# Rotary embedding on one core: one unit's stores moved beside the loads, another's gathered into a single late transfer

## The chip, the cores and the metric

One core of a Trainium2 chip. The time is the device time of one execution in microseconds (us). A profiled execution's span is some 1.8 us shorter than its time. A run is called slow only when it lies over 1.5% above the fastest of its kernel.

A "unit" is 16 of the 64 heads: 4 MiB of float32, as 128 partitions of 8192 elements. There are four, numbered 0 to 3. X0 to X3 are their inputs in SBUF, OUT is the tile that is stored.

## The reference

```python
# x: (8, 8, 1024, 64) float32; freqs: 32; positions: 1024; scale 0.5
angles = np.outer(positions * scale, freqs)
cos, sin = np.cos(angles), np.sin(angles)
out_first  = x_first * cos - x_second * sin      # halves of the last axis
out_second = x_first * sin + x_second * cos
```

16.8 MB come in and 16.8 MB go out, all in float32. Little arithmetic is done per byte.

## The kernel before

GpSimd issues nearly all loads; they cast float32 to float16 on the way. Two quarters of unit 0 are loaded uncast, by SyncE and ScalarE. VectorE works in float16, ScalarE casts back to float32 into OUT, and the stores follow.

```python
    pin(nc.gpsimd.dma_start(out=Xf[0][:, :NH], in_=xv[0][:, :NH]))
    ...                                                   # (cut)
    for u in range(1, NU):
        c = C2 if u == NU - 1 else 0                      # C2 = 1024
        pin(nc.gpsimd.dma_start(out=Xf[u][:, : N - c], in_=xv[u][:, : N - c]))
        if c:
            pin(nc.gpsimd.dma_start(out=Xf[u][:, N - c :], in_=xv[u][:, N - c :]))
    ...                                                   # (cut: the sin/cos table T)
    for u in range(NU):                                   # NU = 4
        OUT = xout.tile([P, N], FP32, tag="O")            # three buffers
        for s in range(2):
            ...                                           # (cut: four VectorE instructions)
            pin(nc.scalar.copy(out=OUT[:, ns], in_=Xf[u][:, ns]))
            if u >= NU // 2:
                pin(nc.sync.dma_start(out=ov[u][:, ns], in_=OUT[:, ns]))
        if u < NU // 2:
            c = C1 if u == 0 else 0                       # C1 = 512
            if c:
                pin(nc.gpsimd.dma_start(out=ov[u][:, :c], in_=OUT[:, :c]))
            pin(nc.gpsimd.dma_start(out=ov[u][:, c:], in_=OUT[:, c:]))
```

So units 0 and 1 are stored by GpSimd, behind the loads in the same queue (q0), and units 2 and 3 in halves by SyncE (q1).

Of the kernel before, what the change touches and what calls it, by code (L numbers as in the profile page):

```python
# [21 lines left out]
def kernel(  # L22
# [8 lines left out]
    nc = tc.nc  # L31
    pin = tc.keep_in_program_order
# [9 lines left out]
    NU = NBH // HEADS  # L42
# [2 lines left out]
    K8 = S // P  # L45
    G = P // HP
    W = K8 * half
    C1 = 512
    C2 = 1024
    assert S % HP == 0 and D == 2 * half and NBH % HEADS == 0 and G * K8 == K  # L50

# [3 lines left out]
    ov = out.rearrange("b h s d -> (b h s d)").rearrange("(u p n) -> u p n", p=P, n=N)  # L55
# [34 lines left out]
        out=one, in_=one, compare_op=ALU.not_equal, fill=1.0, base=0,  # L90
        pattern=[[-1, G], [-G, HP]], channel_multiplier=1,
    ))
    for u in range(1, NU):
        c = C2 if u == NU - 1 else 0
# [11 lines left out]
        out=posf, in_=pos_i64.bitcast(I32).rearrange("p (k t) -> p k t", t=2)[:, :, 0]  # L106
# [3 lines left out]
        out=y,  # L110
# [8 lines left out]
        out=r, in0=m, scalar=_MAGIC, in1=y, op0=ALU.subtract, op1=ALU.subtract  # L119
# [5 lines left out]
        out=ra.bitcast(I32), in0=r.bitcast(I32), scalar1=0x7FFFFFFF, scalar2=None, op0=ALU.bitwise_and  # L125
# [5 lines left out]
    for g in range(0, G, 2):  # L131
        ps = spread.tile([P, 2, 2, W], FP32, tag="g")
        for i in range(2):
            nc.tensor.matmul(  # L134
                out=ps[:, i].rearrange("p t w -> p (t w)"),
# [12 lines left out]
    for u in range(NU):  # L148
        OUT = xout.tile([P, N], FP32, tag="O")
        for s in range(2):  # L150
            ks = slice(s * KH, (s + 1) * KH)
            ns = slice(s * NH, (s + 1) * NH)
            Xs = X[u][:, ks]
            sin_b = T[:, 0, ks].unsqueeze(2).broadcast_to((P, KH, 2, half))
            cos_b = T[:, 1, ks].unsqueeze(2).broadcast_to((P, KH, 2, half))
            pr = tmp.tile([P, KH, 2, half], FP16, tag="pr")
            pin(nc.vector.tensor_tensor(out=pr, in0=Xs, in1=sin_b, op=ALU.mult))  # L157
            pin(nc.vector.tensor_tensor(out=Xs, in0=Xs, in1=cos_b, op=ALU.mult))  # L158
            pin(nc.vector.tensor_tensor(  # L159
                out=Xs[:, :, 0, :], in0=Xs[:, :, 0, :], in1=pr[:, :, 1, :], op=ALU.subtract  # L160
            ))
            pin(nc.vector.tensor_tensor(  # L162
                out=Xs[:, :, 1, :], in0=pr[:, :, 0, :], in1=Xs[:, :, 1, :], op=ALU.add
            ))
            pin(nc.scalar.copy(out=OUT[:, ns], in_=Xf[u][:, ns]))  # L165
            if u >= NU // 2:
                pin(nc.sync.dma_start(out=ov[u][:, ns], in_=OUT[:, ns]))
        if u < NU // 2:
            c = C1 if u == 0 else 0
            if c:  # L170
                pin(nc.gpsimd.dma_start(out=ov[u][:, :c], in_=OUT[:, :c]))  # L171
            pin(nc.gpsimd.dma_start(out=ov[u][:, c:], in_=OUT[:, c:]))  # L172


# [1 line left out]
_INS = ['x', 'freqs', 'positions', 'scale']  # L176
_OUTS = [((8, 8, 1024, 64), 'float32')]
# [30 lines left out]
```

## Time and profile before

| | before |
|---|---|
| time, median of 3 (range) | 84.54 us (84.37 to 84.59) |
| span of the profiled execution | 82.7 us |
| DMA packets of the three queues, share of 16 engines' span | 97.2% |
| VectorE busy / ScalarE busy | 73% / 49% |
| last cast of ScalarE ends | 73.5 us |
| last store lands | 81.8 us |

Read the third row first: the sixteen DMA engines have hardly any free time. The chain on the page names VectorE, because it follows instructions and ends at the last cast, 8 us before the last store has landed. The lines themselves are in the prediction.

### The profile page before, as it was taken

The numbers are of one execution on the slowest core, as the hardware profiler recorded it, in microseconds if no ns is written. First come the engines' busy times: TensorE is split into PE (matmuls) and PEld (weight loads), VectorE is DVE, ScalarE is ACT, GpSimd is POOL, SyncE is SP. The second block draws the span as 40 slices with busy tenths as digits, with TensorE's granted clock in tenths as the row PEclk, the third lists the DMA queues.
The fourth block names the chain that finished last, engine by engine and source line by source line (L and its number), as shares of the span: only waits on it lengthen the run. The fifth ranks groups of instructions, "written<-read, shape, count | busy, mean of one in ns | idle before, by whom it ended". The sixth has DMA issues, their size and how long they took to land.

```text
span 82.7 us, 184 instructions
## 1 busy us (share of the span) xinstructions
PE 6.4 (8%) x18; PEld 2.4 (3%) x18; DVE 60.3 (73%) x40; ACT 40.1 (49%) x18; POOL 5.7 (7%) x16
## 2 busy tenths in 40 slices
PE   0011798200000000000000000000000000000000
PEld 0011232000000000000000000000000000000000
DVE  0306276999999999999999999999999997000000
ACT  0602159999960691294089049309705912950000
POOL 4950000000020002000000200000000000000000
PEclk9999999995555555555555555555555555555555
DMA  3899998996998999999499889989899899999991
GB/s 55 323 323 269 297 325 186 254 254 135 246 254 182 198 254 222 222 222 222 36 456 446 357 386 476 507 357 460 380 523 404 365 428 428 460 404 436 428 428 79
DMA packets 2099, 26.22 MB, mean 317 GB/s; under 512 B 371, under 2 KB 371, under 8 KB 563
## 3 DMA queue, kind: packets, MB, share of 16 engines
q0 software_dynamic: 1088, 15.73, 66.7%
q1 hardware_dynamic: 720, 9.44, 27.3%
q10 hardware_dynamic: 290, 1.06, 3.2%
q14 instruction: 1, 0.00, 0.0%
HBM read 16.79 MB, written 16.78 MB: 406 GB/s over the span
## 4 chain that ended last, share of the span: by engine, by line
DVE 54%; ACT 14%; issue 7%; DMA 6%; PE 5%; DVEq 1%; ACTq 0%
DVE X L158 19%; DVE pr L157 19%; DVE X L162 9%; DMA freq_row<-in_freqs_dram 6%; ACT T L144 5%; DVE X L159 5%; ACT OUT L165 4%; PE ps L134 4%; ACT X L145 4%; DVEq L203 1%; PE cfreq L102 1%; ACT tab L127 1%; DVE r L118 1%; DVE y L109 1%; ACTq L71 0%
## 5 line engine op out<-in xcount | busy, mean ns | idle before, releaser
L165 ACT CAST OUT<-X 128x4096 f32<-128x4096 f16 x8 | 28.8, 3605 | 24.2 <-DVE X L162 24.2
L157 DVE TENSOR_TENSOR pr<-X,T 128x4096 f16<-128x4096 f16 x8 | 18.3, 2292 | 1.0 <-ACT T L144 0.7
L158 DVE TENSOR_TENSOR X<-X,T 128x4096 f16<-128x4096 f16 x8 | 18.3, 2292 | 0.3
L159 DVE TENSOR_TENSOR X<-X,pr 128x2048 f16<-128x2048 f16 x8 | 9.8, 1225 | 0.3
L162 DVE TENSOR_TENSOR X<-pr,X 128x2048 f16<-128x2048 f16 x8 | 9.7, 1218 | 0.0
L144 ACT CAST T<-ps 128x1024 f16<-128x1024 f32 x6 | 5.7, 1030 | 2.6 <-PE ps L134 2.6
L134 PE MATMUL ps<-tab,sel 128*128 128x512 f16 x16 | 5.8, 503 | 2.6 <-ACT tab L127 2.2
L142 DVE CAST T<-ps 128x1024 f16<-128x1024 f32 x2 | 2.4, 1224 | 2.2 <-PE ps L134 2.2
L145 ACT CAST X<-X0f 128x4096 f16<-128x4096 f32 x1 | 3.6, 3650 | 0.0
L100 DVE COPY sel<-one 128x2048 f16<-128x2048 f16 x1 | 0.7, 694 | 2.8 <-POOL one L89 2.8
L122 ACT ACTIVATE tab<-r 128x256 f16<-128x256 f32 x1 | 0.4, 416 | 4.4 <-DVE r L118 4.4
L172 POOL DMA_DIRECT2D out_dram<-OUT x2 | 1.1, 531 | 20.2 <-ACT OUT L165 20.2
L122 ACT ACT_TABLE_LOAD x1 | 1.3, 1283 | 2.1 <-issue 2.1
L134 PEld LDWEIGHTS <-sel 128*128 128x128 f16 x16 | 1.9, 122 | 6.1 <-issue 5.7
L95 POOL DMA_DIRECT2D X<-in_x_dram x3 | 2.0, 658 | 0.0
L171 POOL DMA_DIRECT2D out_dram<-OUT x1 | 0.6, 554 | 19.1 <-ACT OUT L165 19.1
L105 DVE CAST posf<-pos_i 128x8 f32<-128x8 int32 x1 | 0.2, 173 | 2.2 <-DMA pos_i<-in_positions_dram 2.2
L102 PE MATMUL cfreq<-freq_row,coef 1*128 1x32 f32 x2 | 0.6, 391 | 5.9 <-DMA freq_row<-in_freqs_dram 5.9
L109 DVE TENSOR_TENSOR y<-posf,cfreq 128x256 f32<-128x256 f32 x1 | 0.4, 420 | 0.7 <-PE cfreq L102 0.7
L85 POOL DMA_DIRECT2D X<-in_x_dram x1 | 0.7, 669 | 0.8 <-POOLq L189 0.8
L102 PEld LDWEIGHTS cfreq<-freq_row,coef 1*128 1x128 f32 x2 | 0.5, 308 | 5.9 <-issue 5.9
L97 POOL DMA_DIRECT2D X<-in_x_dram x1 | 0.6, 557 | 0.0
(12 smaller groups left out, 2.8 us busy)
## 6 DMA issues: line engine op xcount, KB each, us to landing
out_dram<-OUT SPq DMA_DIRECT2D x4, 2048.0 KB, 11.6
X<-in_x_dram POOLq DMA_DIRECT2D x2, 2048.0 KB, 24.2
out_dram<-OUT POOLq DMA_DIRECT2D x1, 4096.0 KB, 20.4
out_dram<-OUT POOLq DMA_DIRECT2D x1, 3840.0 KB, 21.1
X<-in_x_dram POOLq DMA_DIRECT2D x1, 1792.0 KB, 37.5
X0f<-in_x_dram SPq DMA_DIRECT2D x1, 1024.0 KB, 4.7
X<-in_x_dram POOLq DMA_DIRECT2D x1, 1024.0 KB, 11.5
X0f<-in_x_dram ACTq DMA_DIRECT2D x1, 1024.0 KB, 13.4
```

The source lines that it names most:

```text
L95: pin(nc.gpsimd.dma_start(out=Xf[u][:, : N - c], in_=xv[u][:, : N - c]))
L102: nc.tensor.matmul(out=cfreq, lhsT=coef, rhs=freq_row, start=True, stop=True)
L122: pin(nc.scalar.activation(out=tab[:, 0], in_=r, func=AF.Sin, bias=0.0, scale=-_TWO_PI_DN))
L134: nc.tensor.matmul(out=ps[:, i].rearrange("p t w -> p (t w)"), lhsT=sel[:, g + i].rearrange("s h q -> s (h q)"), rhs=tab.rearrange("s t k ...
L142: pin(nc.vector.tensor_copy(out=dst, in_=ps))
L144: pin(nc.scalar.copy(out=dst, in_=ps))
L145: pin(nc.scalar.copy(out=Xf[0][:, NH:], in_=X0f[:, :NH]))
L157: pin(nc.vector.tensor_tensor(out=pr, in0=Xs, in1=sin_b, op=ALU.mult))
L158: pin(nc.vector.tensor_tensor(out=Xs, in0=Xs, in1=cos_b, op=ALU.mult))
L159: pin(nc.vector.tensor_tensor(out=Xs[:, :, 0, :], in0=Xs[:, :, 0, :], in1=pr[:, :, 1, :], op=ALU.subtract))
L162: pin(nc.vector.tensor_tensor(out=Xs[:, :, 1, :], in0=pr[:, :, 0, :], in1=Xs[:, :, 1, :], op=ALU.add))
L165: pin(nc.scalar.copy(out=OUT[:, ns], in_=Xf[u][:, ns]))
```

## The change

The intent: let unit 0's output leave while loads are still coming in, in turns on another queue, and let unit 2 go out as one large transfer. The diff:

```diff
-    C1 = 512
     C2 = 1024
 ...
             pin(nc.scalar.copy(out=OUT[:, ns], in_=Xf[u][:, ns]))
-            if u >= NU // 2:
+            if u in (0, NU - 1):
                 pin(nc.sync.dma_start(out=ov[u][:, ns], in_=OUT[:, ns]))
-        if u < NU // 2:
-            c = C1 if u == 0 else 0
-            if c:
-                pin(nc.gpsimd.dma_start(out=ov[u][:, :c], in_=OUT[:, :c]))
-            pin(nc.gpsimd.dma_start(out=ov[u][:, c:], in_=OUT[:, c:]))
+        if u not in (0, NU - 1):
+            pin(nc.gpsimd.dma_start(out=ov[u], in_=OUT))
```

## The prediction

> **What bounds the kernel now.** I began with the page's lines of busy tenths and of queues, because the change touches nothing but transfers. They are these.
>
> ```profile
> DVE  0306276999999999999999999999999997000000
> ACT  0602159999960691294089049309705912950000
> DMA  3899998996998999999499889989899899999991
> GB/s 55 323 323 269 297 325 186 254 254 135 246 254 182 198 254 222 222 222 222 36 456 446 357 386 476 507 357 460 380 523 404 365 428 428 460 404 436 428 428 79
> ...
> q0 software_dynamic: 1088, 15.73, 66.7%
> q1 hardware_dynamic: 720, 9.44, 27.3%
> q10 hardware_dynamic: 290, 1.06, 3.2%
> ```
>
> DMA is busy from the second slice to the last but one, also in the last six slices, where VectorE has already ended. The three queues' packets add up to 66.7 + 27.3 + 3.2 = 97.2% of the sixteen DMA engines' span. The chain on the page is a chain of VectorE (54%), but it ends at 73.5 us with ScalarE's last cast. What sets the end is the DMA backlog.
>
> The step of the GB/s line near its middle is not a change of speed. The loads from GpSimd cast f32 to f16, and the line counts what lands. On q0 the stores are 8 MiB (8.39 MB) and the cast loads land 15.73 - 8.39 = 7.34 MB out of 14.68 MB read. So q0 moved 8.39 + 14.68 = 23.07 MB in 66.7% of 16 x 82.7 us = 883 engine-us, and q1 moved 9.44 MB in 361 engine-us: 26.1 KB per engine-us for both. **A byte costs the same as a cast load, as a store from GpSimd and as a store from SyncE.** The windows say the same in time:
>
> ```profile
> 24.00:40.00 16.00, 0.00 (x0) 0.00 (x0) 15.76 (x10) 7.24 (x3) 1.08 (x2) 0.50 1.03 213
> 44.00:52.00 8.00, 0.00 (x0) 0.00 (x0) 7.89 (x5) 4.56 (x2) 0.53 (x1) 0.50 1.02 439
> 53.00:66.00 13.00, 0.00 (x0) 0.00 (x0) 12.79 (x9) 6.75 (x2) 0.00 (x0) 0.50 1.00 431
> 67.00:80.00 13.00, 0.00 (x0) 0.00 (x0) 2.80 (x3) 3.60 (x1) 0.00 (x0) 0.50 1.01 431
> ```
>
> The last two columns are the DMA share and the landed GB/s. Cast loads alone: 213, so 426 read. Stores of GpSimd alone: 439. Both queues together: 431. SyncE's queue alone: 431. There is no gap to fill, and no mixture of queues that was faster than one queue. What no stretch shows is a load beside a store: today q0 is first in, first out, so the loads come first (the last landing at 4.64 + 38.3 = 42.9 us) and unit 0's stores follow behind them.
>
> **What the Trainium skill says.**
> - "DMA: Bandwidth & Descriptors", section "Issuing engines are not separate DMA queues": transfers from all issuers share the same 16 engines, and more issuers save only issue time. The trace agrees: 439, 431 and 431 GB/s above.
> - The same page, "Queues, rings and completion order": each engine takes turns between its queues, packet by packet. The trace agrees. From 53 to 66 us the DMA view gives q0 (32 KB packets) 65.4% and q1 (16 KB packets) 34.7%, near two to one.
> - The same page, "Latency and other measured facts": first byte after about 0.6 us from SyncE and about 1 us from GpSimd. The trace differs. SyncE's first load is issued at 0.74 us and packets begin near 1.7 us, so 1.0 us. GpSimd's first is issued at 1.25 us, and the DMA view of 1.5 to 4.75 us shows no packet of q0, while that of 4.75 to 5.25 has sixteen: 3.5 us. It was a first one, with four more being issued behind it, so I take 3.5 us as the high end.
> - "SBUF — State Buffer", "Who interferes with whom": a VectorE instruction in a 2-port mode keeps GpSimd from writing descriptors; a tensor_tensor has no such mode and, the page infers, does not. During the moved issues VectorE runs tensor_tensor only. No view of this trace tests it, since every late store of GpSimd was hidden behind a backlog.
>
> **The change, part by part.**
> 1. Removed: unit 0's two stores from GpSimd (512 columns, issued at 24.3; the rest at 31.5 us). Two issues of 0.53 to 0.55 us go, on an engine that is otherwise idle: 0 us.
> 2. Added: unit 0's halves from SyncE, after the casts that end at 24.0 and 31.2 us; two issues of 0.33 us on an idle engine: 0 us. They now alternate with the loads of X2 and X3. Total bytes are equal, 33.6 MB, so at equal cost per byte the backlog at any moment is equal too: 0 us, if a load beside a store costs what each costs alone.
> 3. Loads become later. At worst all of unit 0's 4.19 MB go ahead of them: 4.19 MB / 0.432 MB per us = 9.7 us. Landings now: X1 at 2.7 + 19.8 = 22.5 us, before the first store, so unmoved; X2 at about 3.6 + 28.5 = 32.1; X3 at 41.6, its last slice at 42.9. At worst, then, 41.8 and 52.6. The timeline shows when VectorE first reads them, and the casts that release the stores:
>
> ```profile
> 48.73 2.29 DVE L157 TENSOR_TENSOR pr<-X,T 128x4096 f16<-128x4096 f16 x1
> ...
> 55.77 3.61 ACT L165 CAST OUT<-X 128x4096 f32<-128x4096 f16 x1 [3.44 <-DVE X L162]
> ...
> 62.82 2.29 DVE L157 TENSOR_TENSOR pr<-X,T 128x4096 f16<-128x4096 f16 x1
> ```
>
> X2 is wanted at 48.7 and X3 at 62.8 us: slack of 6.9 and 10.2 us. The output buffer that unit 3 takes over is unit 0's, whose store ends near 52 us at the latest, wanted at 62.9. Sum: 0 us.
>
> 4. Unit 2's store is the part that can cost. Today its halves are issued from SyncE at 52.35 and 59.40 us. Now one 4 MiB transfer leaves GpSimd when the second cast ends, 55.77 + 3.61 = 59.4 us. Until then only loads and the stores of units 0 and 1 exist. When do they run out? Counted from the end: SyncE waits 4.8 us between the landings of the last two stores,
>
> ```profile
> SPq L203 <- DMA out_dram<-OUT: 7.5, 2, 4.8
> ```
>
> which is 2.10 MB / 4.8 us = 437 GB/s, so unit 2 and unit 3 take 8.39 MB / 0.432 = 19.4 us. The last store lands at 73.5 + 8.3 = 81.8 us. The DMA view of 67 to 83 us has the last packets begin by 81.0 us, and 16 KB at 26.8 KB per us take 0.6 us, so they stop near 81.4. 81.4 - 19.4 = 62.0 us: by then unit 2's packets must have begun. They begin at 59.4 + 1.0 = 60.4 us if GpSimd starts as fast as SyncE did, at 59.4 + 3.5 = 62.9 us if as slowly as its own first one. The gap is 0 to 0.9 us. I enter +0.2 us.
>
> 5. The tail. Unit 3's halves come at 66.4 and 73.5 us as before, now beside unit 2's remainder on the other queue. From 62.0 us on there are 19.4 us of work; unit 2 alone keeps the engines busy to 71.7 us, unit 3's first half to 76.5, and the last half is there at 74.5. No second gap. Leaving out the 256 KB slice saves one completion, at most 0.1 us.
>
> Sum: 0 + 0 + 0 + 0.2 + 0 = +0.2 us, and +0.1 us for a load beside a store being perhaps slightly dearer, on 84.54: **84.8 us**.
>
> **The rivals.**
> - *Loads and stores overlap in the DMA engines, and the kernel gets faster.* For it: no stretch of today's trace mixes directions, and cast loads write only half of what they read. Against it: a cast load and a store take the same time per byte on the longer side, which looks like one path that both use. And it would gain little. VectorE's chain, with idle times of about 1 us, still ends the last cast at 73.5 us; the last 2 MiB needs 1.0 us to start, 4.9 us of packets and 0.4 us to land, 79.8 us against 81.8. So at most 2.0 us, 82.5 us, and only if nothing else is left then. But unit 2 is not there before 60.4 us, and 19.4 us of stores follow: 79.8 + 0.4 = 80.2, at best 1.6 us less, 82.9 us. A gain above 2% (below 82.85) is nearly shut out.
> - *Unit 2's late store starves the engines.* For it: one transfer where there were two, the first 7 us earlier; only about 2.6 us between the cast's end and the end of the backlog; GpSimd's first start took 3.5 us, and VectorE is busy throughout. Against it: that start was a cold one. At 3.5 us the time becomes 84.54 + 0.9 = 85.4 us; if descriptors wait for one more VectorE instruction of 2.29 us, it is 87.7 us.
> - *A load beside a store is dearer.* Up to 8.4 MB (unit 0 and as many bytes of loads) or about 20 us would run mixed; 5% dearer is +1.0 us, 85.5 us. It would also fill the gap of the second rival, so the two do not add up.
> - *The later loads stall VectorE.* Against it: the 6.9 and 10.2 us of part 3, already at the worst order.
>
> **Range and chances.** The low end is the first rival at about a third of its strength, 84.0 us; the high end is the gap of 0.9 us with a further half microsecond of mixing, or 86.0. Slower by over 2% means above 86.23 us, a gap of 1.7 us: GpSimd would need 4.3 us from the cast to the first packet, or the mixture 8% more. I give that 0.11, faster 0.03, and within 2% 0.86.
>
> **What would show it.** Part 2: two unit-0 stores from SyncE near 24.1 and 31.3 us that take 15 to 21 us to land, against about 20 today; over 24 to 45 us the DMA share stays at 1.0. A sum of read and written bytes clearly above 432 GB/s there would prove the first rival. Part 3: X2 lands between 32 and 42, X3 between 42 and 53 us, and VectorE's instructions keep their start times to 0.2 us; an idle time ahead of a pr, ended by the load of X, would prove the fourth rival. Part 4: GpSimd's issue at 59.4 us, and the DMA share of 60 to 64 us, which tells the gap directly: full means none. Part 5: the DMA share stays at 1.0 from 64 us to within 1.5 us of the span's end. The prediction would be wrong if the engines pause for over 1.7 us after unit 1's store, or if packets of the mixed stretch last longer than those of today.

## The result, and the profile after

| | before | after | after, measured again |
|---|---|---|---|
| median (range) | 84.56 us (84.37 to 84.61) | 84.29 us (84.16 to 84.56) | 84.52 us (84.34 to 84.67) |
| ratio to before, 95% interval | | 0.9976 (0.9958 to 0.9995) | 0.9999 (0.9987 to 1.0011) |

A ratio is the mean time of one kernel's fast runs over that of the other's fast runs of the same rounds, so it is not quite the ratio of the medians. The second measurement had a median of 84.52 us for the ten fast runs of the kernel before beside it. The first one's 0.24% did not come back there; the two together allow no claim but "the same".

The changed kernel's DMA and queue lines on its page (packets, MB landed, share of 16 engines):

```profile
DMA  2899997996996999899899899997995998989992
GB/s 44 345 312 286 282 350 167 255 255 143 239 255 127 255 255 334 302 308 280 239 322 266 239 398 330 545 430 334 509 509 255 509 509 350 414 382 469 422 414 95
...
q0 software_dynamic: 1008, 15.73, 66.5%
q1 hardware_dynamic: 720, 9.44, 27.5%
q10 hardware_dynamic: 290, 1.06, 3.3%
```

The step in the middle of the GB/s line has become a slope: from 28.4 us on, stores (which land what they read) lie among cast loads (which land half). The shares still add up to 97.3%, against 97.2% before, of a span that differs by 0.3 us. The bytes of each queue are even the same, for 4 MiB of stores went from GpSimd to SyncE and 4 MiB went back. Work was rearranged inside a full schedule.

The turns between the two queues do not begin at once. SyncE issues unit 0's first half at 23.86 us, but its first packet begins at 28.45 us, 4.6 us later; the view of 24 to 28 us shows three load packets for each engine and nothing else:

```profile
q0 software_dynamic: 48, 0.79, 108.0%
```

Unit 3's first half waits as long behind unit 2 (66.30 to 71.14 us), and in the kernel before unit 2's first half waited 3.4 us behind GpSimd's stores (52.35 to 55.78 us). The engines were at work meanwhile, so it cost nothing here. The transfers of the mixed stretch, 28 to 48 us of the changed kernel:

```profile
q0 software_dynamic: 192, 2.62, 61.6%
q1 hardware_dynamic: 208, 3.15, 37.5%
```

q0 carries only cast loads here, so 2 x 2.62 MB were read, and 3.15 MB were stored: 8.39 MB in 20 us, 420 GB/s. Cast loads alone were read at 426 GB/s before, stores alone ran at 431 to 439. These views count a packet whole where it starts, so their rates are off by a few per cent (the 439 stands at a share of 1.02). The packet records have no such edges. A load packet of 16 KB landed took 1.23 us before and 1.24 us on average here, a SyncE packet of 16 KB stored 0.611 us alone and 0.623 us here: a load beside a store is as dear as each alone, or 1 to 2% dearer. No overlap shows. (Both kernels have some slow load packets, 11 of 1.79 us at 38 to 39 us before, 36 of 1.53 us at 25 to 33 us after. Above the usual that is 0.5 and 0.7 us of the sixteen engines' time; no run explains them.)

When the stores of each issuer landed, after their issue (minimum, median, maximum over the line's transfers). First SyncE's four in the changed kernel, then GpSimd's two:

```profile
L166 SPq DMA_DIRECT2D out_dram<-OUT x4: 333/333/343, 23.9 to 73.3; - x4
DMA to landing us min/median/max: 8.2/14.2/20.7
```

```profile
L168 POOL DMA_DIRECT2D out_dram<-OUT x2: 533/537/541, 45.4 to 59.5; - x2
DMA to landing us min/median/max: 12.9/14.8/16.7
```

Unit 0's second half, issued at 31.1 us, is the 20.7: it lands at 51.8 us, against 31.5 + 21.1 = 52.6 us for the larger piece before. GpSimd's first is unit 1: 45.4 + 16.7 = 62.1 us. Its second is unit 2, issued at 59.5 us, while unit 1 still had 2.6 us to go.

### The profile page after: what moved, and what is told of

It is laid out like the page before. It is cut to its first block, busy times and chain, and to the rows that moved or that the text cites. A ratio compares the mean times of both kernels' runs of the same rounds, so it can differ in the third digit from the quotient of the medians.

```text
span 82.4 us, 183 instructions
## 1 busy us (share of the span) xinstructions
PE 6.0 (7%) x18; PEld 2.4 (3%) x18; DVE 60.3 (73%) x40; ACT 40.1 (49%) x18; POOL 5.1 (6%) x15
## 4 chain that ended last, share of the span: by engine, by line
DVE 54%; ACT 15%; issue 7%; DMA 6%; PE 5%; DVEq 1%; ACTq 0%
DVE X L157 20%; DVE pr L156 20%; DVE X L161 9%; DMA freq_row<-in_freqs_dram 6%; ACT T L143 5%; DVE X L158 5%; ACT OUT L164 4%; ACT X L144 4%; PE ps L133 4%; DVEq L197 1%; PE cfreq L101 1%; ACT tab L126 1%; DVE r L117 1%; DVE y L108 1%; ACTq L70 0%
## 5 line engine op out<-in xcount | busy, mean ns | idle before, releaser
L168 POOL DMA_DIRECT2D out_dram<-OUT x2 | 1.1, 537 | 53.7 <-ACT OUT L164 53.7
L126 ACT ACTIVATE tab<-ra,quarter 128x256 f16<-128x256 f32 x1 | 0.5, 507 | 0.0
## 6 DMA issues: line engine op xcount, KB each, us to landing
X<-in_x_dram POOLq DMA_DIRECT2D x1, 1792.0 KB, 44.6
X<-in_x_dram POOLq DMA_DIRECT2D x1, 256.0 KB, 47.7
```

## The experiments

All were compared with runs of the kernel before on the same chip. Two theories at the start. **A**: sixteen full DMA engines set the time, and only bytes, and gaps in the work on offer, count; with a rider, that small transfers cost some time too. **B**: alternating stores with loads is worth something in itself.

### The parts of the change one at a time

The kernel before without its 512-column slice:

```diff
-            c = C1 if u == 0 else 0
+            c = 0
```

> The kernel before with unit 0 stored in one piece from GpSimd (the 512-column slice gone, nothing else). Theory A (the sixteen DMA engines are full and only the bytes count; the small gain of the change is the small-transfer overhead it removes): 84.3 to 84.5 us, like the changed kernel. Theory B (the small gain is from mixing stores with loads): 84.56, ratio 1.000 to the kernel before.

Measured: 84.52 us, ratio 1.0013 (0.9997 to 1.0028). The slice is worth nothing. So theory A's rider, that small transfers cost time here, has no support from this run.

Unit 0 beside the loads, unit 2 as before:

```diff
-            if u >= NU // 2:
+            if u == 0 or u >= NU // 2:
                 pin(nc.sync.dma_start(out=ov[u][:, ns], in_=OUT[:, ns]))
-        if u < NU // 2:
-            ...
+        if u == 1:
+            pin(nc.gpsimd.dma_start(out=ov[u], in_=OUT))
```

> Only the first part of the change: unit 0 in halves from SyncE beside the loads; unit 2 still in halves from SyncE. Theory A and B both: 84.2 to 84.4 us (A because the slice is gone too). Rival C (a load beside a store is dearer, and the change hides that by something else): 84.8 us or more.

Measured: 84.85 us, ratio 1.0047 (1.0024 to 1.0070): slower by half a per cent, where both A and B had the changed kernel's time. It looked like rival C, the dearer mixture. But the whole change contains this mixture too and does not pay for it.

Unit 2 whole from GpSimd, unit 0 as before:

```diff
-            if u >= NU // 2:
+            if u == NU - 1:
 ...
-        if u < NU // 2:
+        if u < NU - 1:
```

> Only the second part: unit 2 whole from GpSimd at about 59.4 us; unit 0 as before with its slice. If the backlog of stores covers the start of that transfer, 84.5 to 84.6 us and the DMA share stays at 1.0 from 58 to 66 us. If the late single store leaves a gap, up to 0.9 us more: 85.4 us, with the share below 0.9 near 62 us.

Measured: 84.39 us, ratio 0.9988 (0.9975 to 1.0001). The late single store leaves no gap that the time shows.

### Other pieces

The changed kernel with X3 loaded in one piece, and the kernel before with neither slice (this one also has the edit of the store's slice above):

```diff
-        c = C2 if u == NU - 1 else 0
+        c = 0
```

> The changed kernel with the last unit's load in one piece instead of 7 MiB eighths plus a slice of 1024 columns. Theory A: no more than 0.1 to 0.3 us less (84.0 to 84.2), since X3 is wanted at 62.6 us and lands near 52. If the slice was there to steady something else, 84.3 or more.

Measured: 84.21 us, ratio 0.9976 (0.9960 to 0.9992), in the measurement of the first three experiments. The slice is not needed. The 0.24% stands here too, on another chip than that of the repeat below.

> The kernel before without both small slices (unit 0's store and the last load in one piece each). Theory A (small transfers cost about 1 us around 40 to 43 us in the kernel before, where the last load packets took 1.5 instead of 1.08 us): 83.8 to 84.2 us. If the loss is at the change from loads to stores itself, whatever the pieces: 84.4 to 84.6 us.

Measured: 84.50 us, ratio 1.0008 (0.9994 to 1.0023). Together with the run without the store's slice this ends the idea that small transfers cost the kernel before a microsecond: A's rider is refuted.

### How long a late store takes to start

The larger of my prediction's two positive terms was the gap that might open before unit 2's store. In the changed kernel the start is hidden, so the engines had to be made idle. Both runs store only 512 columns of unit 1, which gives a wrong result. The first issues unit 2 from GpSimd, the second from SyncE:

```diff
-            pin(nc.gpsimd.dma_start(out=ov[u], in_=OUT))
+            w = 512 if u == 1 else N
+            pin(nc.gpsimd.dma_start(out=ov[u][:, :w], in_=OUT[:, :w]))
```

```diff
+            w = 512 if u == 1 else N
+            eng = nc.gpsimd if u == 1 else nc.sync
+            pin(eng.dma_start(out=ov[u][:, :w], in_=OUT[:, :w]))
```

> The changed kernel with only 512 columns of unit 1 stored (a wrong result on purpose), so that the DMA engines have nothing to do when unit 2 is issued from GpSimd at 59.4 us. It measures the time from that issue to the first packet. The end is that first packet plus 19.5 us of stores. Start as fast as SyncE's first load (1.0 us): 83.0 us. Start as slow as GpSimd's first load (3.5 us): 85.5 us. If VectorE's instructions hold the descriptors up: first packet only after one of VectorE's instructions has ended, 60.2, 61.4 or 62.6 us.

> As the run with idle engines, but unit 2 whole from SyncE (wrong result on purpose). First packet 1.0 us after the issue, so 83.0 us; the difference to the GpSimd run is the extra start time of a GpSimd store.

Measured: 83.48 us and 83.44 us, ratios 0.9881 and 0.9870. The timeline of the GpSimd run, around the issue (start, duration):

```profile
55.76 3.60 ACT L164 CAST OUT<-X 128x4096 f32<-128x4096 f16 x1 [3.44 <-DVE X L161]
...
58.09 2.29 DVE L157 TENSOR_TENSOR X<-X,T 128x4096 f16<-128x4096 f16 x1
59.66 0.53 POOL L169 DMA_DIRECT2D out_dram<-OUT  x1 [20.59 <-ACT OUT L164]
60.41 1.22 DVE L158 TENSOR_TENSOR X<-X,pr 128x2048 f16<-128x2048 f16 x1
```

In the windows, the columns after the two times are the length, the busy time (and count) on PE, PEld, VectorE, ScalarE and GpSimd, the clock, the DMA share and the landed GB/s. In the changed kernel the engines are at work while the store is issued, and after it:

```profile
58.00:60.00 2.00, 0.00 (x0) 0.00 (x0) 2.00 (x1) 1.19 (x1) 0.52 (x1) 0.50 0.83 360
60.00:64.00 4.00, 0.00 (x0) 0.00 (x0) 3.93 (x4) 1.33 (x1) 0.01 (x1) 0.50 1.06 459
```

The 0.83 is no pause, for these windows too count a packet where it starts: in the packet records at least fifteen engines have a packet at every moment from 52.6 to 75 us. In the GpSimd run the engines stand still until the store has started:

```profile
58.00:60.00 2.00, 0.00 (x0) 0.00 (x0) 1.97 (x2) 1.36 (x1) 0.34 (x1) 0.50 0.00 0
60.00:62.00 2.00, 0.00 (x0) 0.00 (x0) 1.97 (x3) 0.00 (x0) 0.19 (x1) 0.50 0.84 360
```

Cut finer, the view of 60.50 to 60.75 us of the GpSimd run has no packet, and that of 60.75 to 61.00 us has sixteen, one for each engine: 1.1 us after the issue at 59.66. In the SyncE run, issued at 59.48 us, the sixteen begin from 60.31 us on: 0.8 us. But the issue itself is later on GpSimd, too: it begins 0.3 us after the end of the cast that releases it (59.36 us), SyncE's 0.02 us after (59.46 us). From the cast's end to the first packet it is 1.4 us by GpSimd and 0.85 us by SyncE. So GpSimd starts a store half a microsecond later than SyncE, and not the 2.5 us later that the two engines' first loads had suggested.

VectorE was busy for 1.97 of each 2 us with tensor_tensor instructions. GpSimd's issuing instruction took 0.53 us, no longer than the loads' at 3.6 to 5.2 us, when VectorE was idle (0.54 to 0.56 us), and the first packet did not wait for another whole instruction. That the descriptors waited for the end of the running one is not excluded: a tensor_tensor ended at 60.38 us, 0.4 us before the first packet, and so it is in the next run (67.46 and 67.89 us). At most 0.7 us, from the issue to 60.38 us, can have been lost so.

These two runs also bound the whole idea. With nearly all of unit 1's store out of the way, 3.9 MB or 9 us of DMA time, they are only 1.0 us faster than the kernel before beside them (84.46 us): unit 2's cast ends at 59.4 us, and from there 19.4 us of stores follow whatever came before.

### A gap made on purpose

If a backlog covers the start, then a store held back beyond the backlog must cost what it is late. Unit 2 is issued by GpSimd behind unit 3's first half; the result is correct:

```diff
+    late = []                                             # (before the loop)
 ...
-            if u in (0, NU - 1):
+            if u == 0 or (u == NU - 1 and s == 1):
                 pin(nc.sync.dma_start(out=ov[u][:, ns], in_=OUT[:, ns]))
+            elif u == NU - 1:
+                pin(nc.gpsimd.dma_start(out=ov[u][:, ns], in_=OUT[:, ns]))
+                pin(nc.gpsimd.dma_start(out=ov[u - 1], in_=late[0]))
-        if u not in (0, NU - 1):
+        if u == 1:
             pin(nc.gpsimd.dma_start(out=ov[u], in_=OUT))
+        if u == 2:
+            late.append(OUT)
```

> The changed kernel with unit 2's store held back behind unit 3's first half on GpSimd, so both are issued at 66.3 us; all stores complete, result correct. Theory A says that the backlog is empty at 61.5 us, so the engines stand idle from there to 66.3 plus the start time, and the end moves by 4.8 us plus the start time: 90 to 92 us. If the time were set by VectorE's chain and not by the backlog, it would move by less than 2 us.

Measured: 90.56 us, ratio 1.0730 (1.0698 to 1.0762). The windows of this run, columns as above:

```profile
60.00:62.00 2.00, 0.00 (x0) 0.00 (x0) 1.97 (x3) 0.00 (x0) 0.00 (x0) 0.50 0.61 262
62.00:64.00 2.00, 0.00 (x0) 0.00 (x0) 1.97 (x2) 1.11 (x1) 0.00 (x0) 0.50 0.00 0
64.00:66.00 2.00, 0.00 (x0) 0.00 (x0) 1.97 (x2) 2.00 (x1) 0.00 (x0) 0.50 0.00 0
66.00:68.00 2.00, 0.00 (x0) 0.00 (x0) 1.97 (x2) 0.50 (x1) 1.06 (x2) 0.50 0.25 106
```

The DMA share falls to zero at about 62 us, where the prediction had counted the backlog to end, and returns near 67.9 us, 1.1 us after the issue at 66.79. By the packet records the sixteen engines end at 61.84 us on average and begin again at 67.95 us: they are idle for 6.1 us. The time grew by 90.56 - 84.46 = 6.10 us over the kernel before, measured beside it. VectorE's instructions keep their times. This is theory A by its number, and it says how near the change comes: its store is there at 59.5 + 1.1 = 60.6 us, about 1 us before the backlog ends.

### The repeats, and the surplus of unit 2 from SyncE

The last four were run together. First the changed kernel itself, unedited:

> The changed kernel again, beside the three that follow, to see how far it repeats. 84.2 to 84.4 us if its 0.24% are real, 84.5 if they were chance.

Measured: 84.52 us, ratio 0.9999 (0.9987 to 1.0011). The small gain does not repeat.

Then the kernel with unit 0 and unit 2 both in halves from SyncE, unedited too:

> Unit 0 from SyncE with unit 2 still in halves from SyncE, again. Until 52 us its transfers are those of the changed kernel. If its 84.85 us were chance (engines that lag differently in each execution): 84.3 to 84.5. If unit 2 in halves beside unit 1's store costs time: 84.7 to 84.9.

Measured: 84.93 us, ratio 1.0051 (1.0020 to 1.0083). This surplus does repeat. And unit 2 whole, but from SyncE:

```diff
-            pin(nc.gpsimd.dma_start(out=ov[u], in_=OUT))
+            eng = nc.sync if u == 2 else nc.gpsimd
+            pin(eng.dma_start(out=ov[u], in_=OUT))
```

> The changed kernel with unit 2 whole from SyncE instead of GpSimd. If only the bytes count, 84.2 to 84.4 us, as the changed kernel, although SyncE starts 0.4 us sooner, because the backlog lasts to 61.5 us. If it is the issuing engine that made the difference between the changed kernel and the one with halves: 84.7 to 84.9 us.

Measured: 84.75 us, ratio 1.0031 (1.0016 to 1.0046). The same kind of surplus without the halves. Where is it? In part, at least, not in the transfers. The last microsecond with packets of the changed kernel and of the repeat with halves (windows, columns as above):

```profile
80.00:81.00 1.00, 0.00 (x0) 0.00 (x0) 0.00 (x0) 0.00 (x0) 0.00 (x0) 0.50 0.62 262
```

```profile
80.00:81.00 1.00, 0.00 (x0) 0.00 (x0) 0.00 (x0) 0.00 (x0) 0.00 (x0) 0.50 0.61 262
```

The packets run out at the same moment (81.15 and 81.17 us), yet the spans are 82.4 and 82.8 us. These are the fastest executions of the two kernels. The profile of the first run with halves is of its slowest execution, 85.2 us, and there the packets were late as well: they ended at 81.82 us, against 81.45 us in the kernel before.

What differs between the two with equal packets is the closing of the program. SyncE goes through a list of waits, one or two semaphores at a time. First what SyncE waited for in the changed kernel (total us, times, longest), then in the kernel with unit 2 whole from SyncE:

```profile
SPq L197 <- DMA out_dram<-OUT: 7.4, 2, 4.8
```

```profile
SPq L198 <- DMA out_dram<-OUT: 8.3, 1, 8.3
```

In the first, SyncE waits for two landings one after the other, the last of them 4.8 us after the one before it. In the second it makes a single wait of 8.3 us, for the very last landing, and everything else on its list comes later. The records of these waits in the traces give the order. In the changed kernel, the wait for the last store stands last in the list. SyncE and ScalarE issue eight transfers there, and each has a semaphore of its own (numbers 107 to 110 and 115 to 118). A ninth and a tenth transfer take 107 and 108 again. Those stand at the head of the list, so that the last store is waited for first or second, and the rest of the list comes after it: seven more waits in the kernel with unit 2 whole, six in that with halves, about 62 ns each, 0.43 and 0.37 us. The traces of all fourteen profiled runs agree: from the last landing to the end of the span it takes 0.89 to 0.90 us in the ten with six to eight such transfers, 1.26 us in the two with ten, and 1.33 us in the two with nine. The other one with nine is the idle-engine run of SyncE: its packets ended 0.45 us before those of the GpSimd run, at 80.04 against 80.49 us, and its closing gave that back. So the two have the same time, and SyncE's missed its 83.0 us. The longer closing is thus shown. The surplus of the times is 0.23 us with nine and 0.39 to 0.41 us with ten, in medians, so it is of the same size but not in the same order; that the closing is all of it is not shown, and the lagging engines (above) blur it. The change, by sending unit 2 to GpSimd as it takes unit 0 from it, keeps the count at eight.

Last, a candidate with the fewest transfers: units 0, 1 and 2 whole from GpSimd, unit 3 in halves from SyncE, all loads of GpSimd in one piece each.

```diff
-        c = C2 if u == NU - 1 else 0
+        c = 0
 ...
-            if u >= NU // 2:
+            if u == NU - 1:
 ...
-        if u < NU // 2:
-            c = C1 if u == 0 else 0
+        if u < NU - 1:
+            c = 0
```

> Candidate: units 0, 1, 2 whole from GpSimd, unit 3 in halves from SyncE, every load in one piece, no slices: the fewest transfers, and no load ever beside a store. If the alternation of loads and stores is worth anything, slower than the changed kernel: 84.5 us. If only the number of queues in the last stretch matters, 84.2 to 84.4 us.

Measured: 84.49 us, ratio 0.9999 (0.9987 to 1.0012). Without any store beside a load the time is that of the changed kernel beside it (84.52 us). Theory B falls, as far as this measurement resolves, a tenth of a per cent. No correct version that I tried beats both kernels by more than the measurements scatter.

## Why the prediction was right

**What bounds the kernel, and parts 1 and 2** (issues cost nothing; the backlog stays equal): held. Unit 0's halves took 18.1 and 20.7 us to land, as forecast (15 to 21), though the turns between the queues began 4.6 us after the first issue. The first part alone cannot be read cleanly from a time, for the kernel that has it alone also has two transfers too many on SyncE, but the candidate without any mixture has the time of the changed kernel beside it. The mixed stretch moved 420 GB/s. The prediction's 439 GB/s for GpSimd's stores is an edge of its window, whose share is 1.02; it changes nothing in the sum.

**Part 3** (later loads have slack): held. X2 landed at 3.6 + 31.7 = 35.3 us and X3 at 4.1 + 44.6 = 48.7 us, its last slice at 4.6 + 47.7 = 52.3, inside the intervals given. VectorE began unit 2 at 48.53 us and unit 3 at 62.63, 0.2 us earlier than before; that shift is there from the first output cast on (20.23 against 20.42 us) and comes from the start of this execution.

**Part 4** (the late store): the reckoning held, 62.0 us predicted for the end of the backlog, unit 1 landing at 62.1; where a gap was made, the packets ended at 61.84 us on average. The start was mis-sized. I took 1.0 to 3.5 us from the cast's end and entered +0.2 us for a gap; it measured 1.4 us from there and the gap is 0. The 3.5 us belonged to GpSimd's first transfer of the program with four more behind it, and is no measure of a later one.

**Part 5 and the +0.1 us for mixing**: no second gap, and no surplus that the times show. The "at most 0.1 us" for the slice came from no trace; the run without it shows nothing of the kind. So the 84.8 us was 0.3 to 0.5 us too high, which is the two small positive terms and the scatter of the runs. "Within 2%" alone proves little, for it would also have come out with a gap of 1.5 us; what carries the mechanism is the made gap and the packet records.

**The rivals**: overlapping loads and stores, refuted by 420 GB/s and by the candidate; starvation, real as a mechanism (6.1 us when made), absent by about 1 us in the change; the dearer mixture, 1 to 2% in most packets of a 20 us stretch, not visible in the time; stalled loads, absent.

What stays open: why the first measurement of the changed kernel gave 0.24%, its variant with X3 whole the same, and the second measurement, on another chip than the variant's, nothing. A gain of a quarter of a per cent in some measurements is not excluded. In the packet records of the first profiled execution the sixteen engines finish within 0.28 us of each other, in that of the kernel before within 0.39 us, and in other runs up to 0.96 us apart; the slowest one sets the end. I know no reason for its lag.

## What to carry to other kernels

With the DMA engines full from end to end, as here, reordering transfers or changing their issuer moved no time beyond the closing waits; check instead that something is always on offer, by counting the backlog back from the last landing and comparing it with the earliest moment at which the next store can start. The late store was free as long as it arrived before the backlog ended, and cost its full delay beyond it. Measure a start latency on a later transfer and not on the program's first one, count it from what releases the issue, and look at the closing waits too: a ninth and a tenth transfer of SyncE and ScalarE lengthened them by 0.4 us.

## What the Trainium skill lacked or had wrong

- "DMA: Bandwidth & Descriptors", section "Latency and other measured facts": the first byte after about 0.6 us (SyncE) and 1 us (GpSimd). From the issue to the first packet on idle engines the runs show 0.8 us (1.0 for SyncE's first load) and 1.1 us, and 3.5 us for GpSimd's first transfer of the program, of which the page says nothing.
- The same page, section "Where 436 GB/s comes from", says that the HBM side (about 358 GB/s) binds transfers between HBM and SBUF. This core moved 426 GB/s in loads and 431 in stores; the page's own measurement of 425 fits better. Beside that measurement the page says itself that about 358 is a core's part when both cores of a pair stream.
- The pages that I read give no figure for loads and stores at the same time: 420 GB/s in total here, about the rate of either alone. Nor do they say how long a transfer waits for its first turn when another queue is full: 4.6 and 4.8 us here for SyncE's, 3.4 us in the kernel before. Nor do they say that a cast load is paid by the bytes read: 213 GB/s landed, 426 read.
- "SBUF — State Buffer", section "Who interferes with whom", only infers that tensor_tensor does not hold up GpSimd's descriptors. The runs fit that but do not settle it: 1.1 us from issue to packet with VectorE busy 1.97 of 2 us, yet both times 0.4 us after a tensor_tensor had ended.
- None of the pages that I read has the closing waits: in these kernels a ninth transfer of SyncE and ScalarE reuses a semaphore, and six or seven waits of about 62 ns then follow the last landing (1.26 and 1.33 us to the end of the span, against 0.89).
